# The last overflow check, the second norm's row and the order of the expert groups in a top-4-of-32 layer

## The chip, the cores and the metric

The kernel runs on one core of one Trainium2 chip. The metric is device time in microseconds (us) of one execution. The kernel before took 1158.47 us, the median of three runs (1157.69 to 1159.37). The engines are named as in the profile: PE (matrix products), DVE (vector), ACT (scalar), POOL, and SP, which here only issues DMA transfers; q behind a name (SPq) is the engine's instruction queue.

## The reference, cut to what matters

```python
def moe_ffn(h, router_w, router_b, w_gu, b_gu, w_down, b_down):
    logits = (t @ router_w + router_b)                 # t: 256 tokens x 1024
    top_vals, top_idx = lax.top_k(logits, 4)           # of 32 experts
    gates = softmax(top_vals)
    ...
    for each expert:                                   # w_gu 1024 x 2048, w_down 1024 x 1024, all fp32
        gu = t @ w_gu + b_gu
        gate = minimum(gu[:, :1024], 7.0)
        lin = clip(gu[:, 1024:], -7.0, 7.0)
        y = ((lin + 1) * (gate * sigmoid(1.702 * gate))) @ w_down + b_down
        acc += combine[:, expert] * y
...
x = layer_norm(ALPHA * x + g1 * mix_x, ln1_g, ln1_b)
ffn = moe_ffn(modulate(x, sh2, sc2), ...)
return layer_norm(ALPHA * x + g2 * ffn, ln2_g, ln2_b)  # the "second norm"
```

Ahead of it stand the conditioning, neighbourhood attention, spatial gating and the output projection. The whole layer reads about 450 MB from HBM, of which the 32 experts are 403 MB (12 MiB each).

## The kernel before, in words

**Units.** SBUF is cut into NU = 24 units of 1 MiB (128 partitions x 2048 floats). Long-lived tensors each take one (`unit`, L89); all others carry weights. `stream` is a list of all weight transfers in the order of use. `pump(n, keep)` (L121) takes the next transfer from it as long as more than `keep` units are free, and SP issues it; `done` (L135) frees a piece's unit after its last matmul and pumps one more, with `keep = reserve[0]`. So the order of the transfers is fixed, and a transfer is issued when PE has freed a unit for it. All is written in program order, each engine works through its own instructions in that order, and an instruction that waits holds what stands behind it on its engine.

**Groups.** After a front (38 MiB of weights; until about 205 us) come 13 groups of experts: first experts 0 and 1, then the 12 of `PLAN`, which holds experts by their rank in token count. Each group fills PE's 128 columns: a group of one has 128 token places, a pair 64 for each expert, a group of four ("quad") 32 for each. PE's work per group is therefore much alike, while weights are 12, 24 or 48 units. The order before: pair, quad, single, pair, quad, pair, single, quad, pair, pair, quad, pair, pair (groups 0 to 12).

**One group** (`group`, L1281). Four gate/up steps (`gu_step`), each of two halves, a unit per half and expert; `swiglu_gate` reads the bank on DVE, takes ACT's sigmoid and multiplies on DVE; `swiglu_lin` follows; `h_T` transposes on PE and copies on ACT. `down` goes through four pieces of 256 rows x 1024 columns: with the first two on h0, then `h_T(l_1)`, then two on h1; each piece feeds both output banks. The two banks are scaled, and `scatter` (four matmuls, each into one of four short-product banks that rotate, each added by DVE) is left as `pending` to the next group's place `gu1`. Places between steps are called in0, gu0, in1, gu1, in2, gu2, in3; `hooks` fill them. Group 2, a single, carries the four overflow steps a to d at in0 to in3.

**The last group** takes its down weights by column halves instead (`by_cols`): of each half, row pieces by `DOWN_ROWS`, each column piece of 256 rows a DMA of its own with rows of 2 KB, so that the first half is finished, scaled and scattered while the second still arrives; the very last pieces are 128 rows.

**Overflow.** Tokens beyond an expert's places are done in a loop whose count is read from `nit` (`overflow_items`, L1321); here the count is 0, and the branch is passed. It stands ahead of the last group; four units are kept free for the loop's body during group 11 (`reserve[0] = 4`).

**The second norm's rows.** At group 5, two units are taken (`l2_u`, `row_u`), SP loads ln2_g and ln2_b as two 4 KB rows into `row_u` (L1397, L1398), and at in1 and in2 PE spreads them over 128 partitions with products of a row of ones (L1404), which ACT copies into `l2_u`. Two units are kept free for them during group 4.

Of the kernel before, what the change touches and what calls it, by code (L numbers as in the profile page):

```python
# [9 lines left out]
F32 = mybir.dt.float32  # L10
# [8 lines left out]
P = 128  # L19
D = 1024  # L20
# [13 lines left out]
PAIRS = [[a, a + 1] for a in range(2 + N_SINGLE, NE - 16, 2)]  # L34
PLAN = [QUADS[0], SINGLES[0], PAIRS[0], QUADS[1], PAIRS[1], SINGLES[1], QUADS[2], PAIRS[2], PAIRS[3], QUADS[3], PAIRS[4],
        PAIRS[5]]
DOWN_ROWS = (((0, 512), (512, 512)), ((0, 512), (512, 256), (768, 128), (896, 128)))
NU = 24

# [26 lines left out]
def hybrid_layer_kernel(  # L66
# [153 lines left out]

    def group_stream(gid, ranks, by_cols=False):
        n = 2 if ranks is None else len(ranks)
# [10 lines left out]
        def piece(src, a, i, n):  # L233
            def fn(t):
                SP.dma_start(t, expert(src, a)[i])
                return t.rearrange("p (k n) -> p k n", n=n)
            return fn

        def col_piece(a, r0, rows, col, n):
            def fn(t):  # L240
                v = t[:, 0:rows // P * n].rearrange("p (k n) -> p k n", n=n)
                for r in range(r0, r0 + rows, 256):
                    k0, k1 = r // P % 2, min(r // P % 2 + (r0 + rows - r) // P, 2)
                    SP.dma_start(v[:, (r - r0) // P:(r - r0) // P + k1 - k0, :],  # L244
                                 expert(w_dn, a)[r // 256].rearrange("p (k n) -> p k n", k=2)[:, k0:k1, col:col + n])
                return v
            return fn

        for j in range(2):
            for part in range(2):  # L250
                for half in range(2):
                    for a in range(n):
                        stream.append(((gid, part, j, half, a),
                                       piece(w_gu, a, part * 4 + j * 2 + half, 512)))
        if by_cols:
            for nn in range(2):
                for r0, rows in DOWN_ROWS[nn]:
                    for a in range(n):
                        stream.append(((gid, "c", nn, r0, a), col_piece(a, r0, rows, nn * 512, 512)))
        else:  # L260
            for i in range(4):
                for a in range(n):
                    stream.append(((gid, "d", i, a), piece(w_dn, a, i, 1024)))

# [104 lines left out]
    for u in (cin_u, lnx_u):  # L369
# [10 lines left out]
                    channel_multiplier=-1)  # L380
    ones_b = cst.tile([P, P], BF16, name="ones_b")
    G.memset(ones_b, 1.0)

# [4 lines left out]
    keyc = cst.tile([P, 1], F32, name="keyc")  # L388
    fold4 = cst.tile([P, NE], F32, name="fold4")
    for r in range(4):  # L390
# [838 lines left out]

    def down(n, gid, jh, hTt, ys):  # L1230
        w = P // n
        for i in range(2):
            for k in range(2):
                for nn in range(2):
                    for a in range(n):
                        PE.matmul(ys[nn][a * w:(a + 1) * w, :], hTt[:, (2 * i + k) * P + a * w:(2 * i + k) * P + (a + 1) * w],  # L1236
                                  weights((gid, "d", 2 * jh + i, a))[:, k, nn * 512:(nn + 1) * 512],
                                  start=jh == 0 and i == 0 and k == 0, stop=jh == 1 and i == 1 and k == 1)
            for a in range(n):
                done((gid, "d", 2 * jh + i, a))  # L1240
        t2_free(hTt)

    def down_cols(n, gid, hs, nn, bank):
        w = P // n
        for r0, rows in DOWN_ROWS[nn]:
            for k in range(rows // P):
                kk = r0 // P + k
                for a in range(n):
                    PE.matmul(bank[a * w:(a + 1) * w, :], hs[kk // 4][:, kk % 4 * P + a * w:kk % 4 * P + (a + 1) * w],  # L1249
                              weights((gid, "c", nn, r0, a))[:, k, :], start=kk == 0, stop=kk == KT - 1)  # L1250
            for a in range(n):
                done((gid, "c", nn, r0, a))

# [25 lines left out]
    def group(n, gid, cur, sel, hooks):  # L1279
# [22 lines left out]
        if gid == len(groups) - 1:  # L1302
            hs = (h0, h_T(l_1))
            zst2.extend(sm.tile([P, 2, 6], F32, tag="zst", bufs=2, name=nm("zst")) for _ in range(TT))
            down_cols(n, gid, hs, 0, yb[0])
            ys = [scaled(yb[0], 0)]
            scatter(ys, cur[1], [0])
            down_cols(n, gid, hs, 1, yb[1])
            y = scaled(yb[1], 1)
            for t in range(TT):  # L1310
                PE.matmul(sums[t], cur[1][:, t, :], y, start=False, stop=True)  # L1311
                V.bn_stats(zst2[t][:, 1, :], sums[t])  # L1312
            return None
        down(n, gid, 0, h0, yb)
        h1 = h_T(l_1)
        down(n, gid, 1, h1, yb)
        ys = [scaled(yb[nn], nn) for nn in range(2)]
        return lambda: scatter(ys, cur[1])
# [28 lines left out]
    for gi, rk in enumerate(groups):  # L1347
# [33 lines left out]
        if gi == 1:  # L1381
            hooks["in0"] += [lambda: acc_init((0, 1))]
            hooks["gu0"] += [lambda: acc_init((2, 3))]
            reserve[0] = 1
        if gi == 2:
            ovf_u = unit("ovf")
            reserve[0] = 0
            for k, f in zip(("in0", "in1", "in2", "in3"), overflow_steps(ovf_u[:, 0:512])):
                hooks[k] += [f]
        if nxt:  # L1390
            hooks["gu2"] += [fetch]
        if gi == 4:
            reserve[0] = 2
        if gi == 5:
            l2_u, row_u = unit("l2"), unit("row")
            reserve[0] = 0
            SP.dma_start(row_u[0:1, 0:D], ln2_g)  # L1397
            SP.dma_start(row_u[0:1, D:2 * D], ln2_b)  # L1398
            V.memset(l2_u[0:1, 2 * D - P:2 * D], 1.0)

            def spread(js):
                for j in js:
                    b = ax_bank()
                    PE.matmul(b, l2_u[0:1, 2 * D - P:2 * D], row_u[0:1, j * 512:(j + 1) * 512], start=True, stop=True)  # L1404
                    S.copy(l2_u[:, j * 512:(j + 1) * 512], b)
            hooks["in1"] += [lambda: spread((0, 1))]
            hooks["in2"] += [lambda: spread((2, 3))]
        if gi == 6:
            release(row_u)
            pump(1)  # L1410
        if gi == len(groups) - 2:
            reserve[0] = 4
        if gi == len(groups) - 1:
            pending()
            hooks["gu1"].remove(pending)
            overflow_items()
            hooks["in2"] += [last_sums]
            reserve[0] = 0
            pump(NU)
        pending = group(n, gi, cur, sel_now, hooks)  # L1420
        if gi == 2:
# [24 lines left out]
def _laid_out(inputs):  # L1446
# [9 lines left out]
    a["exp_w_gu"] = a["exp_w_gu"][0].reshape(NE, 2, 4, P, 2, 2, 512).transpose(0, 4, 5, 1, 3, 2, 6).reshape(NE, 8, P, 2048)  # L1456
    a["exp_w_down"] = a["exp_w_down"][0].reshape(NE, 4, 2, P, D).transpose(0, 1, 3, 2, 4).reshape(NE, 4, P, 2048)
    return a
# [23 lines left out]
```

## Time and profile before

| | |
|---|---|
| median of 3 runs | 1158.47 us |
| the profiled execution | 1159.04 us |
| its span, first to last instruction | 1157.3 us |
| PE busy | 1011.2 us (87%) |
| DVE, ACT, POOL busy | 311.0, 137.7, 40.1 us |
| moved by DMA | 449.76 MB, mean 389 GB/s |
| DMA queues | q1 (SP) 448.85 MB; q8 and q14 instruction fetch 0.89 MB; q10 (ACT) 0.02 MB |

Times in the rows are us from the span's start. The page cuts the span into 40 slices of 28.9 us. A timeline row is start, duration, engine, line, operation, out<-in, shapes and count; in brackets the engine's idle time before it and what ended it. Equal instructions of an engine that follow each other are one row: for SP's issues a row runs from the first issue to the end of the last. The group starts in PE's timeline are the first matmul of line 972 (the bias) in each group.

### The profile page before, as it was taken

How to read it: one execution, taken by the hardware profiler on the slowest of the kernel's cores; microseconds unless marked ns; L12 is line 12 of the kernel's file. 1: busy time of each engine (PE TensorE's matmuls, PEld its weight loads, DVE VectorE, ACT ScalarE, POOL GpSimd, SP SyncE). 2: the span in 40 equal slices, each digit the busy share in tenths (PEclk: the TensorE clock that was granted, in tenths of full speed). 3: DMA queues.
4: the chain of work that ended last, by engine and by line, in shares of the span. 5: the costliest groups of instructions: out<-in, count | busy, mean ns of one | idle time of the engine just before them, and what ended most of it. 6: DMA issues, size and time to landing. Idle time of an engine off the chain costs nothing. (4 is left out here: it accounts for less than half of the span.)

```text
span 1157.3 us, 13460 instructions
## 1 busy us (share of the span) xinstructions
PE 1011.2 (87%) x5225; PEld 427.9 (37%) x5225; DVE 311.0 (27%) x621; ACT 137.7 (12%) x297; POOL 40.1 (3%) x72
## 2 busy tenths in 40 slices
PE   6999998999779999976759999879999777689995
PEld 4798555443213534221114353213434112124221
DVE  5687756313103121210111212102121111012114
ACT  4344343110000101000001010000101000000000
POOL 3300301000000000000000000000000000000000
PEclk9999998999989999998869999989999989899998
DMA  9977789889999999999998978999999999999985
GB/s 346 372 277 290 303 305 389 301 372 426 426 428 426 427 427 426 427 426 428 427 426 351 427 262 347 425 428 427 427 426 427 427 426 427 427 426 427 426 334 206
DMA packets 68624, 449.76 MB, mean 389 GB/s; under 512 B 8495, under 2 KB 9663, under 8 KB 15565
## 3 DMA queue, kind: packets, MB, share of 16 engines
q1 hardware_dynamic: 68534, 448.85, 94.2%
q8 instruction: 42, 0.69, 0.2%
q14 instruction: 24, 0.20, 0.0%
q10 hardware_dynamic: 24, 0.02, 0.0%
HBM read 447.80 MB, written 1.05 MB: 388 GB/s over the span
## 5 line engine op out<-in xcount | busy, mean ns | idle before, releaser
L1192 PE MATMUL mm<-w,xg 128*32 128x512 f32 (+2 forms) x2048 | 419.2, 616 | 37.2 <-DMA w<-in_exp_w_gu_dram 37.1
L1236 PE MATMUL mm<-w,t 128*32 128x512 f32 (+2 forms) x960 | 226.2, 695 | 54.1 <-DMA w<-in_exp_w_down_dram 45.4
L1192 PEld LDWEIGHTS mm<-w,xg 128*32 128x32 f32 (+2 forms) x2048 | 128.2, 130 | 314.7 <-issue 236.6
L1236 PEld LDWEIGHTS mm<-w,t 128*32 128x32 f32 (+2 forms) x960 | 62.8, 140 | 205.7 <-issue 108.2
L1276 DVE TENSOR_TENSOR t<-mm,late 128x512 f32<-128x512 f32 x26 | 18.0, 692 | 271.2 <-PE mm L1236 256.3
L1215 DVE TENSOR_SCALAR t<-mm 128x512 f32<-128x512 f32 x26 | 18.0, 692 | 244.9 <-PE mm L1192 244.9
L1208 ACT ACTIVATE t<-t 128x512 f32<-128x512 f32 x26 | 16.4, 630 | 519.2 <-DVE t L1206 519.2
L1206 DVE TENSOR_SCALAR t<-mm 128x512 f32<-128x512 f32 x26 | 18.0, 691 | 201.3 <-PE mm L1192 201.3
L972 PE MATMUL mm<-bgu,sel 32*128 32x512 f32 x104 | 58.2, 639 | 1.3 <-DVEq L1324 1.3
L1259 PE MATMUL ax<-t,sT 128*128 128x512 f32 x100 | 46.2, 604 | 0.8 <-DVE t L1276 0.8
L270 POOL TENSOR_TENSOR rs<-rs,mhalf 128x1 f32<-128x1 f32 x12 | 10.0, 836 | 1056.4 <-DVE mv L282 931.6
L1227 ACT COPY t<-ax 128x512 f32<-128x512 f32 x26 | 15.0, 577 | 260.6 <-PE ax L1223 260.6
L966 PE MATMUL ax<-oh,tM 128*128 128x128 f32 x384 | 44.8, 275 | 0.0
L966 PEld LDWEIGHTS ax<-oh,tM 128*128 128x128 f32 x384 | 43.8, 192 | 0.0
L1261 DVE TENSOR_TENSOR xin<-xin,ax 128x512 f32<-128x512 f32 x50 | 33.2, 684 | 5.0 <-PE ax L1259 4.6
L467 DVE TENSOR_TENSOR wlo<-w,whi 128x1024 fp32r<-128x1024 f32 x20 | 30.1, 1540 | 3.5 <-ACT whi L464 3.5
L1259 PEld LDWEIGHTS ax<-t,sT 128*128 128x128 f32 x100 | 18.1, 189 | 28.9 <-issue 23.5
L972 PEld LDWEIGHTS mm<-bgu,sel 32*128 32x128 f32 x104 | 15.3, 183 | 31.7 <-issue 20.4
L858 ACT ACTIVATE xg<-ax,sh,sc 128x128 f32<-128x128 f32 x60 | 22.5, 459 | 32.8 <-PE ax L966 26.8
L1404 PE MATMUL ax<-row,l 1*128 1x512 f32 x8 | 5.7, 851 | 20.5 <-DMA row<-in_ln_g_dram 20.5
L464 ACT CAST whi<-w 128x1024 fp32r<-128x1024 f32 x20 | 20.1, 1049 | 9.4 <-PE mm L499 9.4
L1223 PEld LDWEIGHTS ax<-ident,t 128*128 128x128 f32 x104 | 11.2, 140 | 21.8 <-issue 18.5
(286 smaller groups left out, 788.0 us busy)
## 6 DMA issues: line engine op xcount, KB each, us to landing
w<-in_exp_w_gu_dram SPq DMA_DIRECT2D x256, 1024.0 KB, 19.4
w<-in_exp_w_down_dram SPq DMA_DIRECT2D x120, 1024.0 KB, 19.5
w<-in_w_front_dram SPq DMA_DIRECT2D x38, 1024.0 KB, 7.1
w<-in_exp_w_down_dram SPq DMA_DIRECT2D x14, 512.0 KB, 11.3
xin<-in_x_dram SPq DMA_DIRECT2D x2, 512.0 KB, 3.9
cin<-in_ctx_dram SPq DMA_DIRECT2D x2, 512.0 KB, 8.4
w<-in_exp_w_down_dram SPq DMA_DIRECT2D x4, 256.0 KB, 9.4
out_dram<-xin SPq DMA_DIRECT2D x4, 256.0 KB, 2.0
```

The lines of the kernel that those rows point to most:

```text
L464: S.copy(av[:, k], w[:, k])
L467: V.tensor_tensor(bv[:, k], w[:, k], av[:, k].bitcast(F32), op=ALU.subtract)
L858: S.activation(dst[:, kk, :], src, AF.Identity, scale=sc2[:, kk:kk + 1], bias=sh2[:, kk:kk + 1])
L966: PE.matmul(bank[:, k * P:(k + 1) * P], late["tMv"][:, t, (hh * 4 + k) * P:(hh * 4 + k + 1) * P], oh[:, t].rearrange("p n w -> p (n w)"), ...
L972: PE.matmul(b, sel[r, :], bgu[r, :], start=True, stop=False)
L1192: PE.matmul(b[a * w:(a + 1) * w, :], xg[:, half * 4 + k, a * w:(a + 1) * w], weights((gid, part, j, half, a))[:, k, :], start=False, stop= ...
L1206: V.tensor_scalar_min(gtile, b, 7.0)
L1215: V.tensor_scalar(lt, b, 7.0, -7.0, op0=ALU.min, op1=ALU.max)
L1236: PE.matmul(ys[nn][a * w:(a + 1) * w, :], hTt[:, (2 * i + k) * P + a * w:(2 * i + k) * P + (a + 1) * w], weights((gid, "d", 2 * jh + i, a) ...
L1259: PE.matmul(b, st[:, t, :], ys[nn], start=True, stop=True)
L1261: V.tensor_tensor(sl, sl, b, op=ALU.add)
L1276: V.tensor_tensor(y, bank, late_v["g2"][:, nn * 512:(nn + 1) * 512], op=ALU.mult)
```

## The change

- `PLAN`: the order becomes pair, quad, single, pair, quad, single, pair, pair, quad, pair, pair, pair, quad; the last group is a quad.
- NU is 26. Room for it comes from a smaller `dynamic_dma_scratch_size` (256), from `ones_b` as a broadcast of one column, and from `fold4` inside `front_u`.
- Down weights are stored by column halves in HBM (the host's layout `_laid_out`): a block of 512 rows x 512 columns is 1 MiB with 8 KB in a row for each partition. All groups load and use them so: first half on h0, `h_T(l_1)`, first half on h1, scaled, then the second half. The last group cuts its second half into 512, 256, 128 and 128 rows, one DMA each.
- `overflow_items` and the pending scatter ahead of it stand before group 5, a single; four units are kept in group 4 for it. Behind it the halves of `xg` and the rotating tiles are stepped once, to keep their parity.
- The second norm's rows are loaded at the start of group 2, straight into `l2_u`, by two DMAs on ACT's queue; the spread comes in group 4, with a broadcast of `ident[0:1, 0:1]` for the row of ones. `row_u` is gone; two units are kept free in group 1 (for `ovf_u` and `l2_u`) where one was.

```diff
@@ -32,10 +32,10 @@
 QUADS = [list(range(a, a + 4)) for a in range(NE - 16, NE, 4)]
 SINGLES = [[2 + i] for i in range(N_SINGLE)]
 PAIRS = [[a, a + 1] for a in range(2 + N_SINGLE, NE - 16, 2)]
-PLAN = [QUADS[0], SINGLES[0], PAIRS[0], QUADS[1], PAIRS[1], SINGLES[1], QUADS[2], PAIRS[2], PAIRS[3], QUADS[3], PAIRS[4],
-        PAIRS[5]]
+PLAN = [QUADS[0], SINGLES[0], PAIRS[0], QUADS[1], SINGLES[1], PAIRS[1], PAIRS[2], QUADS[2], PAIRS[3], PAIRS[4],
+        PAIRS[5], QUADS[3]]
 DOWN_ROWS = (((0, 512), (512, 512)), ((0, 512), (512, 256), (768, 128), (896, 128)))
-NU = 24
+NU = 26
 
 
...
@@ -236,14 +236,11 @@
                 return t.rearrange("p (k n) -> p k n", n=n)
             return fn
 
-        def col_piece(a, r0, rows, col, n):
+        def col_piece(a, r0, rows, nn):
             def fn(t):
-                v = t[:, 0:rows // P * n].rearrange("p (k n) -> p k n", n=n)
-                for r in range(r0, r0 + rows, 256):
-                    k0, k1 = r // P % 2, min(r // P % 2 + (r0 + rows - r) // P, 2)
-                    SP.dma_start(v[:, (r - r0) // P:(r - r0) // P + k1 - k0, :],
-                                 expert(w_dn, a)[r // 256].rearrange("p (k n) -> p k n", k=2)[:, k0:k1, col:col + n])
-                return v
+                k = rows // P
+                SP.dma_start(t[:, 0:k * 512], expert(w_dn, a)[2 * nn + r0 // 512][:, r0 % 512 * 4:r0 % 512 * 4 + k * 512])
+                return t[:, 0:k * 512].rearrange("p (k n) -> p k n", n=512)
             return fn
 
@@ -252,15 +249,10 @@
                     for a in range(n):
                         stream.append(((gid, part, j, half, a),
                                        piece(w_gu, a, part * 4 + j * 2 + half, 512)))
-        if by_cols:
-            for nn in range(2):
-                for r0, rows in DOWN_ROWS[nn]:
-                    for a in range(n):
-                        stream.append(((gid, "c", nn, r0, a), col_piece(a, r0, rows, nn * 512, 512)))
-        else:
-            for i in range(4):
+        for nn in range(2):
+            for r0, rows in DOWN_ROWS[nn if last else 0]:
                 for a in range(n):
-                    stream.append(((gid, "d", i, a), piece(w_dn, a, i, 1024)))
+                    stream.append(((gid, nn, r0, a), col_piece(a, r0, rows, nn)))
 
     group_stream(0, None)
@@ -378,15 +370,16 @@
     G.memset(tri, 1.0)
     G.affine_select(out=tri, in_=tri, compare_op=ALU.is_gt, fill=0.0, base=0, pattern=[[1, P]],
                     channel_multiplier=-1)
-    ones_b = cst.tile([P, P], BF16, name="ones_b")
-    G.memset(ones_b, 1.0)
+    one_b = cst.tile([P, 1], BF16, name="one_b")
+    G.memset(one_b, 1.0)
+    ones_b = one_b.to_broadcast([P, P])
 
     keyb = cst.tile([P, NE], F32, name="keyb")
     G.iota(keyb, pattern=[[-1, NE]], base=NE - 1, channel_multiplier=0, allow_small_or_imprecise_dtypes=True)
     G.iota(keyb[:, 0:2], pattern=[[-1, 2]], base=65536 + NE - 1, channel_multiplier=0,
            allow_small_or_imprecise_dtypes=True)
     keyc = cst.tile([P, 1], F32, name="keyc")
-    fold4 = cst.tile([P, NE], F32, name="fold4")
+    fold4 = front_u[:, 2016:2048]
     for r in range(4):
         q = slice(r * NE, (r + 1) * NE)
@@ -1227,29 +1220,18 @@
         S.copy(t.rearrange("p (k n) -> p k n", n=P), b.rearrange("p (k n) -> p k n", n=P))
         return t
 
-    def down(n, gid, jh, hTt, ys):
+    def down(n, gid, hs, nn, bank, kk0=0, kk1=KT, last=False):
         w = P // n
-        for i in range(2):
-            for k in range(2):
-                for nn in range(2):
-                    for a in range(n):
-                        PE.matmul(ys[nn][a * w:(a + 1) * w, :], hTt[:, (2 * i + k) * P + a * w:(2 * i + k) * P + (a + 1) * w],
-                                  weights((gid, "d", 2 * jh + i, a))[:, k, nn * 512:(nn + 1) * 512],
-                                  start=jh == 0 and i == 0 and k == 0, stop=jh == 1 and i == 1 and k == 1)
-            for a in range(n):
-                done((gid, "d", 2 * jh + i, a))
-        t2_free(hTt)
-
-    def down_cols(n, gid, hs, nn, bank):
-        w = P // n
-        for r0, rows in DOWN_ROWS[nn]:
+        for r0, rows in DOWN_ROWS[nn if last else 0]:
+            if not kk0 <= r0 // P < kk1:
+                continue
             for k in range(rows // P):
                 kk = r0 // P + k
                 for a in range(n):
                     PE.matmul(bank[a * w:(a + 1) * w, :], hs[kk // 4][:, kk % 4 * P + a * w:kk % 4 * P + (a + 1) * w],
-                              weights((gid, "c", nn, r0, a))[:, k, :], start=kk == 0, stop=kk == KT - 1)
+                              weights((gid, nn, r0, a))[:, k, :], start=kk == 0, stop=kk == KT - 1)
             for a in range(n):
-                done((gid, "c", nn, r0, a))
+                done((gid, nn, r0, a))
 
     def scatter(ys, st, nns=range(2)):
@@ -1302,19 +1284,24 @@
         if gid == len(groups) - 1:
             hs = (h0, h_T(l_1))
             zst2.extend(sm.tile([P, 2, 6], F32, tag="zst", bufs=2, name=nm("zst")) for _ in range(TT))
-            down_cols(n, gid, hs, 0, yb[0])
+            down(n, gid, hs, 0, yb[0], last=True)
             ys = [scaled(yb[0], 0)]
             scatter(ys, cur[1], [0])
-            down_cols(n, gid, hs, 1, yb[1])
+            down(n, gid, hs, 1, yb[1], last=True)
             y = scaled(yb[1], 1)
             for t in range(TT):
                 PE.matmul(sums[t], cur[1][:, t, :], y, start=False, stop=True)
                 V.bn_stats(zst2[t][:, 1, :], sums[t])
             return None
-        down(n, gid, 0, h0, yb)
-        h1 = h_T(l_1)
-        down(n, gid, 1, h1, yb)
-        ys = [scaled(yb[nn], nn) for nn in range(2)]
+        hs = [h0]
+        down(n, gid, hs, 0, yb[0], 0, 4)
+        hs.append(h_T(l_1))
+        down(n, gid, hs, 0, yb[0], 4)
+        ys = [scaled(yb[0], 0)]
+        down(n, gid, hs, 1, yb[1])
+        for h in hs:
+            t2_free(h)
+        ys.append(scaled(yb[1], 1))
         return lambda: scatter(ys, cur[1])
 
@@ -1381,42 +1368,37 @@
         if gi == 1:
             hooks["in0"] += [lambda: acc_init((0, 1))]
             hooks["gu0"] += [lambda: acc_init((2, 3))]
-            reserve[0] = 1
+            reserve[0] = 2
         if gi == 2:
-            ovf_u = unit("ovf")
+            ovf_u, l2_u = unit("ovf"), unit("l2")
             reserve[0] = 0
             for k, f in zip(("in0", "in1", "in2", "in3"), overflow_steps(ovf_u[:, 0:512])):
                 hooks[k] += [f]
+            S.dma_start(l2_u[0:1, 0:D], ln2_g)
+            S.dma_start(l2_u[0:1, D:2 * D], ln2_b)
         if nxt:
             hooks["gu2"] += [fetch]
         if gi == 4:
-            reserve[0] = 2
-        if gi == 5:
-            l2_u, row_u = unit("l2"), unit("row")
-            reserve[0] = 0
-            SP.dma_start(row_u[0:1, 0:D], ln2_g)
-            SP.dma_start(row_u[0:1, D:2 * D], ln2_b)
-            V.memset(l2_u[0:1, 2 * D - P:2 * D], 1.0)
-
             def spread(js):
                 for j in js:
                     b = ax_bank()
-                    PE.matmul(b, l2_u[0:1, 2 * D - P:2 * D], row_u[0:1, j * 512:(j + 1) * 512], start=True, stop=True)
+                    PE.matmul(b, ident[0:1, 0:1].to_broadcast([1, P]), l2_u[0:1, j * 512:(j + 1) * 512], start=True, stop=True)
                     S.copy(l2_u[:, j * 512:(j + 1) * 512], b)
             hooks["in1"] += [lambda: spread((0, 1))]
             hooks["in2"] += [lambda: spread((2, 3))]
-        if gi == 6:
-            release(row_u)
-            pump(1)
-        if gi == len(groups) - 2:
             reserve[0] = 4
-        if gi == len(groups) - 1:
+        if gi == 5:
             pending()
             hooks["gu1"].remove(pending)
             overflow_items()
-            hooks["in2"] += [last_sums]
+
+            xg_i[0] ^= 1
+            mo.tile([P, TT, P], F32, tag="sT", name=nm("sT"))
+            mo.tile([P, 1, P], F32, tag="sel", name=nm("sel"))
             reserve[0] = 0
             pump(NU)
+        if gi == len(groups) - 1:
+            hooks["in2"] += [last_sums]
         pending = group(n, gi, cur, sel_now, hooks)
         if gi == 2:
...
-    a["exp_w_down"] = a["exp_w_down"][0].reshape(NE, 4, 2, P, D).transpose(0, 1, 3, 2, 4).reshape(NE, 4, P, 2048)
+    a["exp_w_down"] = a["exp_w_down"][0].reshape(NE, 2, 4, P, 2, 512).transpose(0, 4, 1, 3, 2, 5).reshape(NE, 4, P, 2048)
-    nc = _bacc.Bacc("TRN2", target_bir_lowering=False, num_devices=1)
+    nc = _bacc.Bacc("TRN2", target_bir_lowering=False, num_devices=1, dynamic_dma_scratch_size=256)
```

## Rows read from the trace of the kernel before

**Rows 1.** The page's part 2: GB/s in 40 slices of the span.
```profile
GB/s 346 372 277 290 303 305 389 301 372 426 426 428 426 427 427 426 427 426 428 427 426 351 427 262 347 425 428 427 427 426 427 427 426 427 427 426 427 426 334 206
```

**Rows 2.** Stretches: length, busy time (instructions) of PE to POOL, clock, DMA share, GB/s.
```profile
241.90:602.00 360.10, 302.57 (x1476) 104.42 (x1472) 60.64 (x132) 18.75 (x40) 0.00 (x0) 0.92 1.01 426
602.00:720.00 118.00, 116.54 (x492) 47.87 (x493) 27.50 (x52) 9.35 (x20) 0.00 (x0) 1.00 0.88 348
660.00:705.00 45.00, 44.27 (x172) 20.35 (x174) 9.21 (x16) 3.46 (x8) 0.00 (x0) 1.00 0.75 271
720.00:1090.00 370.00, 316.43 (x1512) 108.46 (x1506) 55.45 (x106) 19.82 (x44) 0.00 (x0) 0.94 1.01 427
1090.00:1115.00 25.00, 25.00 (x104) 7.90 (x102) 3.81 (x6) 1.64 (x3) 0.00 (x0) 1.00 0.83 340
1115.00:1131.00 16.00, 13.12 (x56) 4.12 (x54) 1.73 (x3) 0.68 (x2) 0.00 (x0) 1.00 1.03 391
1131.00:1142.00 11.00, 10.21 (x42) 3.24 (x42) 3.36 (x5) 0.00 (x0) 0.00 (x0) 1.00 0.91 351
```

**Rows 3.** SP's queue, waits (total, times, longest): whole span; 205:242; 1090:1119.
```profile
SPq L235 <- DMA w<-in_exp_w_gu_dram: 301.2, 159, 2.9
...
SPq L235 <- PE mm L1192: 24.6, 6, 8.5
...
SPq L1324 <- SPq L1324: 19.1, 8, 3.6
```

**Rows 4.** Timelines of SP and PE around the spread.
```profile
579.73 0.24 SPq L1398 DMA_DIRECT2D row<-in_ln_b_dram  x1
...
591.73 3.75 PE L1404 MATMUL ax<-row,l 1*128 1x512 f32 x4 [20.48 <-DMA row<-in_ln_g_dram]
```

**Rows 5.** The chain that ended last, its end: start, us, what.
```profile
1137.23 7.07 PE mm L1249 x32
...
1153.59 0.75 DVE xin L1436
```

**Rows 6.** PE's timeline: the first bias matmuls of groups 2, 3 and 4.
```profile
350.31 1.12 PE L972 MATMUL mm<-bgu,sel 32*128 32x512 f32 x2
...
408.50 1.12 PE L972 MATMUL mm<-bgu,sel 32*128 32x512 f32 x2
...
464.06 1.12 PE L972 MATMUL mm<-bgu,sel 32*128 32x512 f32 x2
```

**Rows 7.** The page's part 5: down matmuls, busy and mean, idle before and releaser.
```profile
L1236 PE MATMUL mm<-w,t 128*32 128x512 f32 (+2 forms) x960 | 226.2, 695 | 54.1 <-DMA w<-in_exp_w_down_dram 45.4
```

**Rows 8.** The page's part 6: transfers, KB each, median us from issue to landing.
```profile
w<-in_exp_w_gu_dram SPq DMA_DIRECT2D x256, 1024.0 KB, 19.4
...
xin<-in_x_dram SPq DMA_DIRECT2D x2, 512.0 KB, 3.9
```

**Rows 9.** SP's timeline: issues in groups 2 and 3 (first start, to last end, count).
```profile
350.06 5.23 SPq L235 DMA_DIRECT2D w<-in_exp_w_down_dram  x3
357.42 19.97 SPq L235 DMA_DIRECT2D w<-in_exp_w_gu_dram  x9
...
384.39 16.25 SPq L235 DMA_DIRECT2D w<-in_exp_w_gu_dram  x5
405.17 16.46 SPq L235 DMA_DIRECT2D w<-in_exp_w_down_dram  x8
422.48 15.42 SPq L235 DMA_DIRECT2D w<-in_exp_w_gu_dram  x7
```

**Rows 10.** Timelines of ACT, DVE and PE in group 2.
```profile
359.80 0.63 ACT L1208 ACTIVATE t<-t 128x512 f32<-128x512 f32 x1 [29.50 <-DVE t L1206]
...
361.61 0.48 DVE L1023 TENSOR_TENSOR ohg<-oh,late 128x128 f32<-128x128 f32 x2
363.82 0.15 DVE L1142 CAST nit<-ax 1x1 int32<-1x1 f32 x1 [1.73 <-PE ax L1141]
...
367.25 3.60 PE L1259 MATMUL ax<-t,sT 128*128 128x512 f32 x8
```

More of the change, by code (lines that the diff above doesn't have):

```diff
@@ L219, in hybrid_layer_kernel, with group_stream @@
     stream.extend((key, block(i, n)) for i, (key, _, _, _, n) in enumerate(FRONT))
-    def group_stream(gid, ranks, by_cols=False):
+    def group_stream(gid, ranks, last=False):
         n = 2 if ranks is None else len(ranks)
```

## The prediction

> **What bounds the kernel now.** I read four views in this order: the page's slices, a table of stretches, the waits of PE and of SP's queue, and the timelines around what these pointed to.
>
> The slices say that the transfers set the time [rows 1]: from the tenth slice on they run at 425 to 428 GB/s, and fall below it only in slices 22, 24 and 25 and in the last two. In the stretches [rows 2], 241.9:602 moves 426 GB/s and 720:1090 moves 427, so the weight stream has no room there, whatever PE does. I take 427 GB/s as full rate; a 1 MiB unit then takes 1.0486 MB / 427 GB/s = 2.456 us. What a stretch loses is its length times (1 - rate/427): 602:720 loses 118 x (1 - 348/427) = 21.8 us, of which 660:705 alone 16.4; 1090:1115 loses 5.1; 1115:1131 loses 1.4 and 1131:1142 2.0. The stretch before 241.9 is paced by the units that PE gives back: SP's queue waited 24.6 us for matmuls of line 1192 there [rows 3].
>
> The cause of the middle loss stands in PE's timeline [rows 4]: in group 5 PE sat 20.48 us before the spread of the second norm's rows, because SP had put the two 4 KB row transfers into the stream, the second at 579.73, behind weights already under way. For that time PE freed nothing, the buffers filled, and the group of one behind it kept them full. With the wait gone, what is late next is the stream itself.
>
> The ends: the last weights land near 1142, the last matmul ends at 1137.23 + 7.07 = 1144.30, then come product, statistics and norm, to 1154.34 [rows 5], and the outgoing transfers, to 1157.3. The profiled run took 1159.04, 1.74 more than its span; the median of the runs, 1158.47, is 0.57 below that run.
>
> **The change part by part.** The sum is over transfer time lost.
>
> *The row by ACT's queue: the wait of 20.48 goes.* The rows are issued at the start of group 2, and used in group 4. Does the whole 21.8 go with it? PE is then 20.5 us earlier against the stream, and two more things widen the margin: two units more, and one unit (row_u) not taken. A group of one takes PE 408.50 - 350.31 = 58.2 us for 12 units = 29.5 us of transfers; a pair 55.6 us for 58.9 [rows 6]. So a single lets the stream run ahead by 28.7 us = 11.7 units, and each pair gives back 1.4. After the change 20 units hold weights from group 3 on (26 less xin, tM, xg, late, t2, l2). At the end of a group of four PE eats what lands; 11.7 on top of a few stays under 20. I take -21.8; the bounds are 0 and -21.8, and -5.4 is left if the stretch 660:705 stays as it is.
>
> *26 units for 24.* Up to 241.9 each issue waits for a unit that PE gives back, so two units more mean 2 MiB more moved when the stream becomes continuous: 2 x 2.456 = -4.9. In group 1 two units are kept back for one before, which is covered as the stream has a backlog there. Bounds 0 and -4.9; I take -4.9, as nothing on PE in this stretch waits for weights.
>
> *The end: a group of four, down weights stored by column halves.* Before, the last down pieces go out as 512 KB and smaller transfers with rows of 2 KB, and cost 1.4 + 2.0 = 3.3 us against full rate. After, all but the last 12 pieces (4 of 512 KB, 8 of 256 KB) are whole 1 MiB units of 8 KB rows; the last 4 MiB in rows of 4 and 2 KB cost about 0.8 at the rate of 391. Net -2.5, bounds 0 and -3.3. A group of four needs 117.9 us of transfers, twice a pair's, and it is there that PE waits for weights (45.4 us for down weights in all [rows 7]); so it waits for the last piece too, and the tail of 13 us is the same: one row block behind the last landing. In the other groups the new order of the down matmuls has as many of them, and hides behind transfers; without this cover it would cost at most the wait for h1's copy once more, under 1 us a group.
> The Trainium skill's page "DMA: Bandwidth & Descriptors", section Specifications, puts the size from which a transfer runs at line rate at 512 B; the stretch 1115:1131 with 2 KB rows ran at 391 GB/s while its engines were as busy as at 427, so the measurement decides. By the page, 1.4 of the 3.3 has another cause and may stay, and the sum would be 1135.9.
>
> *The overflow branch moved from before group 12 to before group 5.* SP waits there for everything it has out: 19.1 us in eight waits [rows 3], and the stream loses the 5.1 of 1090:1115. This stall moves with it: 0 net. It comes in a group of one, which SP enters with 16 units issued (12 of them that group's), so PE has its weights throughout; PE's own share (it now waits for the pending scatter first) falls into a group in which the stream gains on it. Four units kept in group 4 leave 16, enough for the backlog of a group of four. Bounds -5.1 and +5.1.
>
> *What the ACT queue costs.* SP never has more than eight transfers out: a transfer takes 19.4 us from issue to landing [rows 8], eight times 2.456, and SP's queue waited 159 times for a landing of gate or up weights [rows 3]. If ACT's two DMAs count in the same eight, in program order, the first stands eight behind the last down unit of the group of one (S0), the second behind the first unit of the pair. 19 units are issued beyond the group of four when group 2 begins, 12 + 7. In the times of the run before these go out at 354.95 (third of the three from 350.06) and 357.42 [rows 9] and land at 374.4 and 376.8. ACT waits till then, and S0's first sigmoid, at 359.80 before [rows 10], comes at about 377.3, 17.5 late. DVE stands behind it with its product; then come 1.7 us of its own work and step_b's copies, which in the run before were at 363.8. PE has four banks for short products: its fourth scatter matmul, due at 367.25 + 3 x 0.9 = 369.95, needs step_b's bank, free at 377.3 + 0.63 + 1.66 + 0.3 + 0.1 = 380.0. PE loses 10.0 us. How much of it reaches the stream: by 445.45 the margin is least. The transfer issued at 384.39 lands at 403.8, the 19 behind it until 445.4 [rows 9] at 403.8 + 46.7 = 450.5, 5.0 after the next issue; a transfer without others takes 3.9 for 512 KB [rows 8], 2.7 over its 1.2, so 2.3 us were to spare, and with one unit more (20 for 19) 4.8. So +5.2. Bounds 0 (ACT is not held) and +10.0 (nothing to spare). No row shows ACT issuing behind other transfers; I take 5.2, as SP's own issues are held like that.
> The Trainium skill's page "DMA: Bandwidth & Descriptors", section "Anatomy of one DMA — SWDGE (gpsimd) path", says that the DMA engines wait on no semaphore and any such wait happens on the issuing sequencer. By this rule ACT itself stands, and the sum is as below; were the wait in the queue, it would be 1129.3. No run here shows it for ACT.
>
> *Edits at nothing.* The broadcast of ones and fold4's place in front_u change operands of a few small instructions. The spread's eight matmuls move to group 4, where PE waits for transfers. The smaller scratch: the page's third part shows no queue but the hardware's own and instruction fetch, so nothing uses it. Uncovered, these are under 1 us together.
>
> Sum: 1157.3 - 21.8 - 4.9 - 2.5 + 0 + 5.2 = 1133.3 span; + 1.74 = 1135.0 as profiled; - 0.57 = 1134.5 against the median.
>
> **The rivals.**
> 1. *ACT is not held* (its DMAs count apart, or the eight before them have landed): 1134.5 - 5.2 = 1129.3. For it: only one ACT DMA in the trace, and it waits for nothing. Against it: SP's waits for landings have one pattern throughout.
> 2. *The change doesn't clear the middle*: buffers fill in the group of one behind the branch, and the loss of 660:705 stays: 1134.5 + 16.4 = 1150.9. For it: that group is where PE is slowest per byte, and SP stands in it. Against it: the margin reckoned above.
> 3. *Slower: down weights by column halves run at the rate of the column pieces.* 128 MiB of them, 134.2 MB, take 314.3 us at 427 and 343.2 at 391: +28.9, so 1163.4. It decides from about 394 GB/s down, where it eats the 24.0 and 2.3 more. For it: the only column pieces in the trace ran at 391. Against it: they had 2 KB rows, and the new layout stores each half so that a partition reads 8 KB in one piece, as the gate and up units do at 427.
>
> **How the numbers follow.** Forecast 0.47, rival 1 0.35, rival 2 0.11, rival 3 0.04, and 0.03 for something I don't see, either way. The range 1126 to 1147 takes in the forecast with ACT's stall at its bound (1139.3), the two units worth nothing on top (1144.2) and the end too (1146.7), and below rival 1 with the branch 3 us cheaper. What a measurement of this kernel can tell from no change is about 0.2%, 2.3 us. Faster: the first three and a part of the rest, 0.93; the same 0.02; slower 0.05.
>
> **What would show it.** Right: no PE wait at the spread; GB/s near 427 from 237 to the last group but for one gap of some 5 us at group 5, in which SP waits for eight landings; 2 MiB more moved by 242. ACT's hold shows as an idle of some 25 us before the first sigmoid of group 2 beside its DMA issues, PE's stop in the scatter there, and a dip of the rate near 440. Wrong: a second dip in groups 5 to 8, a rate of 391 in down weights, or a longer tail behind the last landing.

## The result, and the profile after

The changed kernel took 1145.47 us (median of 4 runs, 1140.13 to 1145.53) against 1158.36 for the kernel before beside it: ratio 0.9877, 95% interval [0.9847, 0.9906]. The forecast was 1134.5, the range 1126 to 1147: side and range held, and the time is 11 us above the forecast. The profiled execution took 1145.53, its span 1143.8.

The slices of the page, which answer to [rows 1]:
```profile
GB/s 341 411 322 285 322 282 402 227 389 422 421 420 421 421 421 421 420 421 422 420 341 424 421 421 420 421 421 422 421 421 421 421 421 422 421 421 421 421 420 195
```
One gap is left, slice 21. But the plateau is 421 where it was 427, from its first slice on. The stretches, to be held against [rows 2] (same columns):
```profile
241.90:570.00 328.10, 292.56 (x1447) 103.58 (x1444) 60.92 (x128) 19.25 (x41) 0.00 (x0) 0.96 1.01 418
570.00:600.00 30.00, 30.00 (x96) 14.61 (x95) 6.63 (x16) 3.50 (x8) 0.00 (x0) 1.00 0.84 344
600.00:720.00 120.00, 117.81 (x510) 45.52 (x510) 25.51 (x49) 8.75 (x19) 0.00 (x0) 1.00 1.01 422
720.00:1090.00 370.00, 317.88 (x1484) 106.63 (x1484) 54.61 (x103) 18.07 (x39) 0.00 (x0) 0.95 1.01 421
1115.00:1129.00 14.00, 12.21 (x65) 3.12 (x66) 3.31 (x5) 0.00 (x0) 0.00 (x0) 1.00 0.91 329
```
602:720 ran at 348 before and 600:720 runs at 422: the middle loss is gone. 720:1090 has the same DMA share, 1.01, as before, and 421 for 427: the DMA engines are as busy and move less. 570:600 is the branch. In PE's timeline the two spreads, where [rows 4] had 20.48 us of idle time, have none:
```profile
473.99 1.98 PE L1385 MATMUL ax<-l,ident 1*128 1x512 f32 x4
...
488.10 1.98 PE L1385 MATMUL ax<-l,ident 1*128 1x512 f32 x4
```
ACT's queue and engine around the two row transfers, and PE's scatter of that group (compare [rows 10]):
```profile
347.68 0.23 ACTq L1377 DMA_DIRECT2D l<-in_ln_g_dram  x1
347.95 0.27 ACTq L1378 DMA_DIRECT2D l<-in_ln_b_dram  x1
357.06 0.63 ACT L1201 ACTIVATE t<-t 128x512 f32<-128x512 f32 x1 [36.18 <-DVE t L1199]
```
```profile
360.97 3.70 PE L1185 MATMUL mm<-w,xg 128*128 128x512 f32 x8
364.51 3.60 PE L1241 MATMUL ax<-t,sT 128*128 128x512 f32 x8
```
The rows went out as the group began, the sigmoid waited for DVE and not for them, and the eight scatter matmuls ran through in 3.60 us: ACT was not held. SP's waits over the whole span (total, times, longest):
```profile
SPq L1311 <- SPq L1311: 19.4, 6, 9.0
...
SPq L242 <- DVE oh L946: 12.8, 1, 12.8
...
SPq L242 <- DMA l<-in_ln_g_dram: 2.5, 1, 2.5
```
The branch's wait is the 19.1 of [rows 3], at its new place. The last row, in group 2, is SP waiting once for a row that ACT's queue brings.

Where the time went, all kernels of this study together. From the packets of each kernel's one profiled execution I took, in us, when 60, 90, 400 and 440 MB had been moved, when the last weight packet was through, and the span. "90-400" is the time between two such marks, "tail" the time from the last weight packet to the end of the span; "units" is the number of units and the remainder of their start address in SBUF by 256 bytes:

```
kernel   units     60MB   90MB   90-400  400-440  440-last  tail   span
before   24, 0    189.0  271.7   749.5   100.1     20.6     15.4  1157.3
after    26, 160  182.7  269.4   742.9    95.1     21.8     14.6  1143.8
a_256    26, 0    186.1  272.6   732.8    93.8     21.6     14.6  1135.4
a_256r   26, 0    182.5  268.9   732.8    93.7     21.8     14.6  1131.8
a_64     26, 192  181.8  265.3   743.3    95.0     22.2     14.7  1140.5
a_128    26, 128  183.6  270.2   742.8    95.0     22.1     14.7  1144.8
b_row    24, 0    187.2  268.4   727.7   102.0     20.9     15.3  1134.3
b_32     24, 32   186.9  268.6   759.3   102.5     21.9     14.8  1167.1
a_24     24, 0    186.9  268.5   732.9    93.7     21.9     14.5  1131.5
a_nobr   26, 0    181.6  264.8   727.8    93.9     22.7     14.6  1123.8
a_pair   26, 0    181.8  265.1   732.8    94.0     21.1     18.4  1131.4
a_sp     26, 0    181.8  265.3   732.9    93.8     21.9     14.6  1128.5
a_mid    26, 0    181.7  264.8   732.8    93.8     21.1     15.7  1128.2
a_fix    26, 0    184.3  267.4   732.1    93.7     21.9     14.6  1129.7
```

### The profile page after: what moved, and what is told of

Read it like the earlier page. It is cut to its first block, busy times and chain, and to the rows that moved or that the text cites. A ratio compares the mean times of both kernels' runs of the same rounds, so it can differ in the third digit from the quotient of the medians.

```text
span 1143.8 us, 13445 instructions
## 1 busy us (share of the span) xinstructions
PE 1016.1 (89%) x5225; PEld 429.4 (38%) x5225; DVE 311.6 (27%) x620; ACT 137.5 (12%) x297; POOL 39.9 (3%) x72
## 5 line engine op out<-in xcount | busy, mean ns | idle before, releaser
L1185 PE MATMUL mm<-w,xg 128*32 128x512 f32 (+2 forms) x2048 | 428.5, 626 | 43.5 <-DMA w<-in_exp_w_gu_dram 43.5
L1231 PE MATMUL mm<-w,t 128*32 128x512 f32 (+2 forms) x1024 | 235.8, 648 | 51.2 <-DMA w<-in_exp_w_down_dram 42.6
L1231 PEld LDWEIGHTS mm<-w,t 128*32 128x32 f32 (+2 forms) x1024 | 67.1, 134 | 207.8 <-issue 110.2
L965 PEld LDWEIGHTS mm<-bgu,sel 32*128 32x128 f32 x104 | 15.5, 185 | 31.3 <-issue 19.9
L1216 PEld LDWEIGHTS ax<-ident,t 128*128 128x128 f32 x104 | 11.2, 141 | 21.8 <-issue 16.8
L593 DVE SCALAR_TENSOR_TENSOR accB<-w,front,accB 128x2048 f32<-128x2048 f32 x8 | 18.8, 2348 | 0.0
```

The lines of the kernel that those rows point to most:

```text
L593: V.scalar_tensor_tensor(accB_u, w[:, 0, :], sT[:, k, 0:1], accB_u, op0=ALU.mult, op1=ALU.add)
L965: PE.matmul(b, sel[r, :], bgu[r, :], start=True, stop=False)
L1185: PE.matmul(b[a * w:(a + 1) * w, :], xg[:, half * 4 + k, a * w:(a + 1) * w], weights((gid, part, j, half, a))[:, k, :], start=False, stop= ...
```

## The experiments

**Where the units lie: a_256, a_64, b_32, a_128.** In the rate's 1.4% lay the main question. The packets told it more closely: those of 8 KB took exactly 309 ns before, and 309 to 322 after, in gate/up and down weights alike. What the change does to all of them is to move the units in SBUF: `one_b` takes 32 bytes for the 256 of `ones_b`, `fold4` gives up 128, the scratch 16128. In the compiled programs the first unit began at byte 26368 of a partition, a multiple of 256, and begins at 9888, 160 past one; units are 8192 bytes apart, so all share it. a_256 pads one small tile ahead of the units:
```diff
-        nb = cst.tile([NE, 1], BF16, name="nb")
+        nb = cst.tile([NE, 64], BF16, name="nb")[:, 0:1]
```


> The changed kernel, with its 26 units moved up by 96 bytes in SBUF, so that each begins at a multiple of 256 bytes instead of at one of 256 plus 160 (nothing else differs). Theory (placement): the weights land 32 bytes off a multiple of 64, and that is why a packet of 8 KB takes 314 ns on the mean instead of 309 and the stream runs at 421 GB/s instead of 427. Then the packets return to 309 ns, the rate to 427, and the 371 MB after 242 us take 12.4 us less: about 1133. Rival (the smaller scratch, the low addresses, or the order of the transfers slows the stream): 421 GB/s as in the changed kernel, 1145. Rival (the chip slows some packets at random): 421 here and there, no difference between the four kernels of this call that follows the placement.

a_64 pads it to 32 elements:

> The changed kernel, with its 26 units moved up by 32 bytes only: each then begins at a multiple of 64 bytes, but not of 256 (remainder 192). Theory (placement, boundary of 64 bytes): 309 ns a packet, 427 GB/s, 1133, as with 256. Theory (placement, boundary of 256 bytes): between, packets still above 309 ns, about 1145. Rival (not the placement): 1145.

b_32 does the reverse to the kernel before, `[NE, 32]` and the small scratch (`dynamic_dma_scratch_size=256`), without which it doesn't fit:

> The kernel before, with the smaller scratch and with its 24 units so placed that each begins 32 bytes past a multiple of 64 (and of 256). Theory (placement): the packets take 314 ns and the stream runs at 421; the stretches in which it sets the pace (242 to 602 and 720 to 1090, 730 us at 427) take 1.4% longer, +10, so about 1168. Rival (the order of the transfers or the chip): 427 GB/s and 1158. If the small scratch did the harm: 1168 as well, and the run with 256 then stays at 1145.

a_128 puts `nb` behind the units instead (`sm.tile`):

> The changed kernel with its units moved down by 32 bytes (one small tile stands elsewhere), so that each begins at a multiple of 128 bytes that is none of 256. What is still open is the boundary: 32 bytes off a multiple of 64, and at a multiple of 64, packets of 8 KB took 314 ns, at multiples of 256 309 ns. If 128 is enough: 309 ns and 427 GB/s in the paced stretches, and some 1131. If it has to be 256: 314 ns, 421 GB/s, and some 1143.

Measured: a_256 1131.95 (ratio 0.9781 [0.9750, 0.9813]), and, measured again (a_256r, below), 1130.43 (0.9772 [0.9752, 0.9793]); a_64 1142.67 (0.9887 [0.9852, 0.9923]); b_32 1171.86 (1.0142 [1.0105, 1.0180]); a_128, one run, 1146.54 beside 1158.16. The 8 KB packets between 760 and 860 us:
```
kernel   start mod 256   mean ns   1st, 50th, 99th percentile
before          0         309.4    309 309 309
a_256           0         309.3    309 309 309
b_32           32         315.0    309 313 321
a_128         128         313.9    309 313 322
after         160         314.1    309 313 322
a_64          192         314.0    309 312 321
```
And 720:1090 in a_256r, then b_32 (columns of [rows 2]):
```profile
720.00:1090.00 370.00, 316.00 (x1522) 107.94 (x1520) 55.97 (x105) 18.65 (x40) 0.00 (x0) 0.97 1.01 427
```
```profile
720.00:1090.00 370.00, 314.64 (x1498) 108.02 (x1499) 53.89 (x104) 19.79 (x44) 0.00 (x0) 0.94 1.01 420
```
The placement is the cause, both ways round, and the order of the transfers and the small scratch are cleared: a_256r has both and runs at 427. Of the two boundaries I had written, 64 fell: it takes 256, and 128 isn't enough. The Trainium skill ("DMA: Bandwidth & Descriptors", How a descriptor splits into AXI transactions) says that transactions are of 256 bytes and must start at a multiple of 256, so that with another start bytes ahead of the piece are fetched as well and cost beats (of 32 bytes). The trace agrees on the boundary. It does not agree on the size: by an estimate from the page's rule, an 8 KB piece of 256 beats takes one beat more with a start 32 off and five more with one 160 off (0.4 and 2.0%), and here 32 off cost most (315.0 for 309.4 ns, 1.8%). The page speaks of reading; here the place written to was moved. Why the packets are slower stays open.

**The row alone: b_row.** The kernel before with `l2_u` taken and the rows issued by ACT at group 2, the spread left in group 5 (cut; the second row likewise, and two units are kept free in group 1 and none in group 4):
```diff
+            S.dma_start(l2_u[0:1, 0:D], ln2_g)
...
-            l2_u, row_u = unit("l2"), unit("row")
...
-            SP.dma_start(row_u[0:1, 0:D], ln2_g)
```


> The kernel before with the change to the second norm's rows alone: they come by ACT's queue at the start of group 2 into one unit, are spread in group 5 as before, and the second unit (row_u) isn't taken; its units stay at multiples of 256 bytes. Theory (the prediction's term): the wait of 20.5 us goes and 21.8 us of transfer time with it: 1158.4 - 21.8 = 1136.6, with 427 GB/s from 602 to 720. Rival (the buffers fill in the group of one behind it all the same): 16.4 stay, 1153. ACT held by the limit of eight transfers out: PE stops some 10 us in group 2's scatter and up to 5.2 are lost there, so 1142; not held: 1136.6.

1137.67 (0.9839 [0.9815, 0.9863]). The stretches of [rows 2]:
```profile
241.90:602.00 360.10, 324.43 (x1591) 117.47 (x1589) 67.93 (x144) 22.79 (x49) 0.00 (x0) 0.96 1.01 427
602.00:720.00 118.00, 111.86 (x508) 44.68 (x508) 22.17 (x44) 8.18 (x18) 0.00 (x0) 0.98 1.01 427
```
From 90 to 400 MB it took 749.5 - 727.7 = 21.8 us less: the forecast's term to the tenth. From 400 to 440 MB, where the branch stands, it took 1.9 more (102.0 for 100.1). By the medians this one edit, 19.9 us beside its own runs of the kernel before, did more than the whole change as it stands, 12.9; the intervals just overlap.

**The other terms, beside the aligned kernel: a_256r, a_24, a_nobr, a_pair.**

> The changed kernel with units at multiples of 256 bytes once more, as the measure for the three beside it: 1132, with 427 GB/s in the stretches that the stream paces.

`NU = 24`:

> The changed kernel with units at multiples of 256 bytes, and 24 units instead of 26. Theory (the prediction's term): 2 MiB less moved when the stream becomes continuous near 242, +4.9 us, so 1137. By the trace of the changed kernel, which had moved 1.6 MB more by 242, it would be +3.8. Rival (the two units also carry the backlog through the groups behind the branch): a stop of PE or a dip of the rate between 560 and 800, and more than +5. Rival (worth nothing, what was ahead is given back at the branch, where all that is out has to land): 1132.

1133.05 (0.9812 [0.9788, 0.9836]): 2.6 us by the medians, not clear of the noise, as the interval overlaps that of a_256r and the two profiled spans are equal within 0.3. Between 90 and 400 MB it is level with 26 units (732.9 and 732.8), so nothing more hangs on them behind the branch.

Without `overflow_items()`:

> The changed kernel with units at multiples of 256 bytes, and without the branch over the overflow loop ahead of group 5 (the loop is left out; with these inputs it runs no time). Theory (the prediction's term: the drain costs 5.1 us of transfers wherever it stands): 1132 - 5 = 1127, and 427 GB/s from 570 to 600 instead of some 350. Rival (the stop is hidden, since a later group waits for its weights for another reason): 1132. Rival (the branch costs PE more than the stream): below 1125.

1125.46 (0.9752 [0.9728, 0.9775]), 5.0 us less by the medians and 5.0 less between 90 and 400 MB (727.8 for 732.8), and the gap closes; a_256r's 570:600, then a_nobr's:
```profile
570.00:600.00 30.00, 30.00 (x100) 15.09 (x98) 6.49 (x16) 2.87 (x7) 0.00 (x0) 1.00 0.87 360
```
```profile
570.00:600.00 30.00, 29.27 (x99) 15.10 (x98) 5.70 (x11) 3.45 (x8) 0.00 (x0) 1.00 1.01 428
```
`QUADS[3], PAIRS[5]]` at the end of the plan:

> The changed kernel with units at multiples of 256 bytes, the last two groups changed over: the group of four is the last but one, a pair ends the order, still with its down weights by column halves and finely cut row pieces (2 of 512 KB and 4 of 256 KB instead of twice as many). Theory (the prediction: at the end of a pair as of a group of four PE waits for the last piece, and what was gained at the end comes from the rows of 4 and 8 KB): 1132, within 1. Rival (the group of four is what the end gains from; behind a pair PE is still at work when the last weights have landed): 1 to 3 us more, with a longer tail behind the last packet.

1132.91 (0.9798 [0.9777, 0.9819]), 2.5 more by the medians (the intervals overlap), and the tail behind the last packet is 18.4 instead of 14.6 us: it is the trace that bears the rival out. PE's last down matmuls in a_pair, whose last packet was through at 1113.0, and in a_256r (1117.2):
```profile
1101.12 7.09 PE L1231 MATMUL mm<-w,t 128*64 128x512 f32 x32
1109.00 1.98 PE L1241 MATMUL ax<-t,sT 128*128 128x512 f32 x4 [0.79 <-DVE t L1258]
1110.91 7.09 PE L1231 MATMUL mm<-w,t 128*64 128x512 f32 x32
```
```profile
1111.90 4.87 PE L1231 MATMUL mm<-w,t 128*32 128x512 f32 x22 [0.18 <-DMA w<-in_exp_w_down_dram]
1116.98 1.68 PE L1231 MATMUL mm<-w,t 128*32 128x512 f32 x4 [0.20 <-DMA w<-in_exp_w_down_dram]
```
In the pair PE waits for no weights and ends 5.0 us behind the last packet (1110.91 + 7.09); in the group of four it waits for each piece and ends 1.4 behind (1118.66).

**Queue, end and front: a_sp, a_mid, a_fix.** `SP.dma_start` for the two rows:

> The changed kernel with units at multiples of 256 bytes, and the second norm's two rows issued at the same place of the program (the start of group 2), by SP's queue instead of ACT's. Theory (it is the early issue that takes the wait away, not the queue): no wait of PE at the spread, 0.977 of the time before, as with ACT's queue (1130 against 1157), within 2 us. Rival (two of the eight transfers that SP has out are then 4 KB small, and the stream is short of them): up to 2 x 2.46 us more, 0.981, with a dip of the rate near 350. Rival (as the forecast had it for ACT, the issue waits for the eight before it and holds what stands behind): the same for SP's own weights, which wait so anyway: nothing.

1130.36 (0.9771 [0.9753, 0.9790]). The instructions on the rows' tile:
```profile
L1385 PE MATMUL ax<-l,ident x8: 587/587/691, 468.6 to 483.8; 1*128 1x512 f32 x8
...
L1377 SPq DMA_DIRECT2D l<-in_ln_g_dram x1: 296/296/296, 368.2 to 368.2; - x1
L1378 SPq DMA_DIRECT2D l<-in_ln_b_dram x1: 244/244/244, 370.5 to 370.5; - x1
```
In SP's line they go out at 368.2 and 370.5, 22 us later than by ACT's queue (345.95 in a_256r), and 98 us before their use at 468.6. The early place is what counts; ACT's queue brought nothing here.

`DOWN_ROWS[1]` ending in `(768, 256)` instead of two of 128:

> The changed kernel with units at multiples of 256 bytes, and the very last row pieces of 512 KB instead of two of 256 KB each (4 transfers instead of 8 at the end). In the kernel it is changed from, the last 8 MB took 21.8 us from the time when 440 MB were moved to the last packet, where 427 GB/s would take some 18, and the last 7.5 us ran at 300 to 325 GB/s. Theory (eight transfers of 256 KB are too little to have out, and so cost rate): the last packet comes 1 to 2 us earlier after the 440 MB, PE's tail behind it is up to 1 us longer, and the time 0.5 to 1 us less (0.976). Rival (rows of 2 and 4 KB cost it, whatever the size of the transfer): the end is the same within 0.5 us and the tail longer, 0.978.

1130.26 (0.9773 [0.9753, 0.9794]): the last packet came 0.7 to 0.8 us earlier after the 440 MB (21.1 for 21.8), and the tail is 1.1 longer (15.7 for 14.6). So the finest pieces do cost something, less than I wrote, and the tail takes it back. This edit doesn't part the size of the transfers from that of their rows, which it doubles (2 KB to 4 KB). The packets say what the rows do: one of 2 KB took 84 ns (median in a_256r), one of 4 KB 159, one of 8 KB 309, so that 512 packets of 4 KB instead of 1024 of 2 KB save 0.3 us over 16 engines. The rest of the 0.7 to 0.8 is left open. (The last 7.5 us before a_256r's last weight packet ran at 246 GB/s, not at 300 to 325.)

Fixed experts for the first group of four, so that its transfers can be listed ahead of the ranking (cut):
```diff
+    group_stream(1, None, es=(2, 3, 4, 5))
...
-            for g2_, rk2 in enumerate(groups[1:], 1):
+            for g2_, rk2 in enumerate(groups[2:], 2):
```


> The changed kernel with units at multiples of 256 bytes, and the first group of four takes the weights of four fixed experts (2 to 5) instead of the four that the ranking names: it leaves out the choice of these experts' weights, so that SP can issue them before the ranks are known. Theory (with 26 units all weights known ahead of the ranks are out by 211 us, and the stream stands for some 8 us between 202 and 219 until SP knows the first ranks, so that two units more bring 2.6 instead of 4.9 us): the stops near 202 to 219 go, and the time falls by 2 to 5 us, 0.973 to 0.975. Rival (PE's returning units sets the pace there in any case): 0.977, and the stops move to where PE returns no unit.

1132.28 (0.9777 [0.9755, 0.9798]): no gain, so my theory fell and the rival held. Stretches with no packet at all between 202 and 222 fell from 8.5 us in a_256r to 1.7, but SP then waits for PE (205 to 242):
```profile
SPq L235 <- PE mm L1186: 21.2, 5, 8.6
SPq L242 <- PE mm L1186: 7.0, 1, 7.0
```

## Why the forecast was right, and where it was wrong

By its own terms, span against span:

```
term              forecast   measured   from
middle             -21.8      -21.8     b_row, 90-400 MB
two units           -4.9       -2.8     90 MB: 268.9 for 271.7, one execution each
end                 -2.5       -0.9     131.0 to 130.1, below
branch               0          0       5.1 before, 5.0 at the new place (a_nobr)
ACT held            +5.2        0       not held
"edits at nothing"   0        +12.0     after - a_256r
```
So 1157.3 - 21.8 - 2.8 - 0.9 = 1131.8, a_256r's span (the branch's 5.1 and 5.0 are taken as equal), and 12.0 more is the 1143.8 of the changed kernel: 0.5 of it before 90 MB, 10.1 between 90 and 400, 1.4 behind.

- *The step that failed* is "Edits at nothing", and with it "I take 427 GB/s as full rate" for the changed kernel. I had looked at what the two operand changes and the scratch do on their engines, and not at where they put the tiles behind them. 371 MB after 242 us at 421 instead of 427 are 371 x (1/0.421 - 1/0.427) = 12.4 us. None of my rivals held it; rival 3 had the right kind of damage, a slower stream, in the wrong transfers: down weights ran at the rate of gate/up. The new layout and order cost nothing there: without the branch in it, 90 to 400 MB took 727.8 us in a_nobr with them and 727.7 in b_row without.
- *ACT held* was wrong, and rival 1 right. Had the units stayed where they were, its 1129.3 would have been the forecast to keep (a_256r 1130.43), with the errors in the units and the end still in it. What failed is the step that counted ACT's rows in SP's eight, in program order: the issue went out as its group began (347.68, first bias product 347.57), although 12 + 7 transfers stand ahead of it in the program. Something does reach across the queues, the other way: SP waited 2.5 us for the landing of the ln_g row.
- *Two units*: the forecast's 4.9 is there at 60 MB (186.9 to 187.2 with 24 units in a_24 and b_row, 181.6 to 182.7 in most with 26), but by 90 MB the executions overlap: 268.4 to 271.7 with 24 units, 264.8 to 272.6 with 26. The -2.8 is a difference of two of them; with a_256, the same program as a_256r, it would be +0.9. What the two units are worth in the end isn't shown beyond a_24's 2.6. Some of it may go where SP stands before the ranks are known, but a_fix, which takes that wait away, gave nothing back. The rest is left open: PE's clock there differs from execution to execution. 180 to 205 us in a_24, then a_256r; the granted clock, third from the right, is 0.93 and 0.72, a mean over its two levels:
```profile
180.00:205.00 25.00, 21.05 (x143) 13.50 (x143) 15.82 (x49) 7.46 (x21) 2.01 (x2) 0.93 0.97 399
```
```profile
180.00:205.00 25.00, 21.30 (x127) 14.18 (x126) 13.46 (x39) 6.16 (x16) 2.00 (x2) 0.72 0.91 375
```
- *The end*: from 400 MB on, 136.1 us, or 131.0 without the branch's 5.1, became 130.1. The last pieces are no faster than the old ones: behind the 440 MB they took 21.8 us for 20.6, where at 427 the 7.8 MB take 18.3, so they lose 3.5 and not the 0.8 reckoned (0.9 by its own figures). The shorter rows are not it: at 84 and 159 ns a packet they cost 0.6, and before, all in rows of 2 KB, 1.6. The DMA engines stood idle instead: over that stretch their share was 0.91, and 0.98 before. "The tail of 13 us is the same" holds from the last down product on: 1157.3 - 1144.3 = 13.0 before, 1131.8 - 1118.7 = 13.1 in a_256r, 13.4 in a_pair. Wrong was that PE waits for the last piece at the end of a pair too. There it was late itself: its last 32 products ran without a break for 7 us [rows 5] and ended 2.4 behind the last landing, for 1.4 with the group of four, which keeps up with the landings.
- *The branch* and *the middle* came as worked out, and rival 2 is out: 600:720 is at the plateau.

That the result lay in the range is partly luck: 12.0 not seen, 5.2 feared and not met, and 3.7 of gain too much in the units and the end: 1133.3 + 12.0 - 5.2 + 3.7 = 1143.8.

## What to carry to other kernels

When the stream is the bound, a small tile added or dropped ahead of the big buffers is a change to every transfer: look up the buffers' start addresses in the two compiled programs, and keep them at multiples of 256 bytes. Price a moved issue by which earlier transfers it must wait for at that time, not by its place in the program. At the end, choose the last group by whether PE can follow the landings, then cut the last pieces. The version to keep is a_256: 1130.4 to 1132.0 us, by the ratios 1.0 to 1.1% below the changed kernel (0.9781 and 0.9772 against 0.9877), for 96 bytes of padding.

## What had not been expected of the hardware

- 8 KB packets into SBUF at 32, 128, 160 or 192 bytes past a multiple of 256 took 313.9 to 315.0 ns on the mean, at a multiple 309.3 to 309.4; over 16 engines 420 to 421 against 427 GB/s. DMA share stays at 1.01: this loss doesn't show as idle time in the stretches.
- As the last pieces of 512 and 256 KB came in, the stream ran at 329 GB/s (1115:1129 of the changed kernel), with a DMA share of 0.91. The packets of a_256r took 84, 159 and 309 ns (medians) for 2, 4 and 8 KB: an estimate from these three is a fixed 9 ns a packet and 37.5 ns a KB.
- One program reached the 90 MB mark at 268.9 us in one profiled execution and at 272.6 in another (a_256r, a_256), with clocks of 0.72 and 0.80 from 180 to 205 us; its nine runs lie between 1127.7 and 1137.1. The higher clock had the later mark, so that mean doesn't order them; what does was not tried, and 3 us between two single runs mean nothing here.
